# Sums of weight quarters: accumulating transfers within SBUF instead of additions on GpSimd

## The chip, the core and the metric

The kernel runs on one core of a Trainium2 chip. A core has TensorE (matrix products into PSUM), VectorE, ScalarE and GpSimd (elementwise work on the on-chip memory SBUF), and SyncE, whose queue here issues transfers. In the profile they are PE (its weight loads PEld), DVE, ACT, POOL and SP; transfers run on 16 engines that all queues share. The metric is the device time of one execution in microseconds. Three runs of the kernel before took 1261.45, 1261.13 and 1259.82 us: median 1261.13.

## The reference

One inference step of a two-layer decoder on 512 prompt tokens and 8 x 8 sample tokens, model width 1024, all in float32. Layer 0 mixes by a gated linear recurrence, layer 1 by attention with a sliding window; each layer ends in a feed-forward part, and the scales and shifts of the normalizations come from a condition vector through further matrices:

```python
def swiglu(h, w_in, w_out):
    gate, up = jnp.split(h @ w_in, 2, axis=-1)
    return (jax.nn.silu(gate) * up) @ w_out
...
        x = x + g1[:, None, :] * out
        h = modulate(rms_norm(x, norm_g[l, 1]), sh2, sc2)
        x = x + g2[:, None, :] * swiglu(h, ffn_w_in[l], ffn_w_out[l])
```

`ffn_w_in` is 1024 x 5632 (gate and up, 2816 columns each), `ffn_w_out` 2816 x 1024. The change lies in the product `h @ w_in` alone.

## The kernel before

The tokens are split into two halves h = 0, 1 of 288 columns each (256 of the prompt, 32 of the samples); activations lie with their features on the partitions. Float32 matrices are multiplied in three passes of a faster format: each operand is split into a rounded part and a remainder, and rounded times rounded, rounded times remainder and remainder times rounded are accumulated in PSUM. For a weight this split is a cast on ScalarE from a tile `raw` (the loaded weights, 4 buffers, line 539) into a tile `wh`, and a subtraction on VectorE for the remainder.

Of the 22 column tiles of `w_in` per layer the first 3 (`PLAIN`, line 1225) are multiplied plainly. The other 19 are taken as *pairs*: tile i of gate and tile i of up, each split by its upper and lower 512 rows, are the four quarters of a 2 x 2 block matrix, and the two token halves, split the same way, are the four quarters of the other. One level of a fast scheme of the Strassen-Winograd kind forms 7 products of quarters in place of 8, at the price of sums of weight quarters and of activation quarters beforehand and of products afterwards. The names of the seven weight operands are 11, 22, S1, S2, 12, S3, S4. In a pair's two `raw` tiles, r11 and r12 are the two halves of the gate's tile, r21 and r22 those of the up tile, and the sums are made in place, one after the other (lines 1284 to 1302): S1 is r21 + r22 in r22, then S3 is r11 - r21 in r21, S2 is S1 - r11 in r11, and S4 is r12 - S2 in r12. These four additions or subtractions per pair, each of 128 partitions x 512 columns, run on GpSimd (`operand`, line 1262); there are 2 x 19 x 4 = 152. After each, `operand` splits the result into one of the ten `wh` buffers (line 540), rounded part and remainder side by side. The `raw` tile of up is free again once S3 is split, that of gate once S4 is split; only then can the load of a later tile go into it.

The pairs are taken in four blocks of 2, 5, 6 and 6 (`GROUPS`, less the 3 plain tiles); after each block come 16 products with `w_out` (8 column tiles, two halves). `queue` (line 1308) lists the operands in the order 11, 22, S1, S2, 12, S3, S4; `pump` (line 1323) makes the next one as soon as one of the ten `wh` is free by the program's count. `emit` (line 1416) uses them in the order S1, S2, 12, 11 of the next pair, S3, S4, 22. `seven` (line 1339) issues a product, 4 blocks of 128 rows in 3 passes, so 12 matmuls, and then the additions that turn products into results: 11 and 12 share a PSUM bank, S2, S3 and 22 another, S1 and S4 a third. Product 11 is copied out as `p1`, S1 as `p5`; S2's bank takes `p1` and is copied to `u2`; Silu makes the gate, VectorE or GpSimd multiplies by up, and `whole` splits the result for the product with `w_out`. `quarters` (line 946) makes the sums of the activations' quarters once per layer, on VectorE, from the quarters b11, b21, b12, b22, and `two` splits them.

Beside this, in layer 0, `ada_pace` spreads the products of the condition vector over the work; their weights (512 KB at a time) are loaded on SP between the weights of the pairs.

The order of instructions on every engine comes from a planner inside the kernel. Each operation is recorded with a cost, an engine and what it reads and writes (`record`, line 430); `schedule` (line 227) then places the operations one after the other by priority, by when their inputs are ready and by when a buffer is free, and the result is emitted as the fixed order of each engine's queue. For a transfer the recorded cost is 1020 ns on GpSimd's queue, and its end is reckoned from its bytes and fixed additions; for an addition on GpSimd it is 150 ns and 2.4 ns per column. Each queue works strictly in order, and waits on semaphores for what an instruction needs.

Of the kernel before, what the change touches and what calls it, by code (L numbers as in the profile page):

```python
# [16 lines left out]
ALU = mybir.AluOpType  # L17
# [10 lines left out]
HC = 288  # L28
# [487 lines left out]
def trunk_kernel(ctx, tc, a):  # L516
    nc = tc.nc
    rec = Recorder(a["shadow"])
    V, S, G, T, Q = (Engine(rec, n, o) for n, o in (("DVE", nc.vector), ("ACT", nc.scalar), ("POOL", nc.gpsimd), ("PE", nc.tensor), ("SP", nc.sync)))
# [10 lines left out]
    def ps(pool=pmm, tag="mm"):  # L530
        cnt[0] += 1
        return rec.tile(pool, tag, NMM if tag == "mm" else (8 - NMM), RMM if tag == "mm" else 1, [P, 512], F32, f"{tag}{cnt[0]}")
# [48 lines left out]
    def split(hi, lo, v):  # L581
        S.copy(hi, v)
        V.tensor_tensor(lo, v, hi.bitcast(F32), ALU.subtract)
# [362 lines left out]
    def quarters(c):  # L946

        if c == 0:
            kinds = [tb] * 8 + [ta] * 3 + [sl] * 13
            X2["kinds"] = kinds  # L950
            for j in (2, 3, 4):
                X2[j] = [None] * 4
        b11, b21, b12, b22 = [V2[h][k] for h, k in ((0, c), (0, c + 4), (1, c), (1, c + 4))]

        def two(j, y):
            X2[j][c] = [X2["kinds"].pop(0)(F32R) for _ in range(2)]
            split(X2[j][c][0].r[:, 0:HC], X2[j][c][1].r[:, 0:HC], y.f[:, 0:HC])
            y.done()

        def minus(o, p, q):  # L960
            V.tensor_tensor(*[y.f[:, 0:HC] for y in (o, p, q)], ALU.subtract)

        minus(b11, b12, b11)
        minus(b12, b22, b12)
        two(3, b12)
        minus(b22, b22, b11)
        minus(b21, b21, b22)
        two(2, b22)
        two(4, b21)

# [26 lines left out]
    def load_more(upto=NRAW):  # L997
        while nload[0] < len(units) and nload[0] - nconv[0] < upto:
            u = units[nload[0]]
            u.raw = raws()  # L1000
            t = u.raw.f[:, 0 : u.kc * P].rearrange("p (k n) -> p k n", n=P)
            for rows, ks, cols, src in u.srcs:
                Q.dma_start(t[rows, ks, cols], src)
            nload[0] += 1
# [53 lines left out]
    def residual(h, o, c, g, last):  # L1058
        xp, xs = x[h][:, c, 0:HP], v48(x[h][:, c, HP:HC])
        V.scalar_tensor_tensor(xp, o[:, 0:HP], mp(g, c), xp, ALU.mult, ALU.add)  # L1060
        t = ta()
        V.tensor_tensor(v48(t.f[:, 0:32]), v48(o[:, HP:HC]), msam(g, c, h), ALU.mult)
        (V if g == L1 + G2 and c == KC - 1 else G).tensor_tensor(xs, xs, v48(t.f[:, 0:32]), ALU.add)
        t.done()
        if last and (g != L1 + G2 or c < KC - 1):
            square(h, c)
# [147 lines left out]
    for m in range(KC):  # L1214
# [3 lines left out]
            lambda h, o, m=m: residual(h, o, m, G1, True),  # L1218
# [8 lines left out]
    def ffn(l, g, after):  # L1227
# [18 lines left out]
        for f in range(PLAIN):  # L1246
            for w, ev in ((0, evac_gate), (1, evac_up(f))):
                c = 2 * f + w
                linear(unit_cols(wi, w * DFF + f * P), hops, ev, lambda h, c=c: quarters(c) if h == 1 and c < 4 else None)

                jobs[-1].late = f == PLAIN - 1
# [9 lines left out]

        def operand(i, name, src, sums=()):
            w = W[i, name] = whs()
            for o, p, q, op in sums:
                G.tensor_tensor(o, p, q, op)
            S.copy(w.r[:, 0:H2], src)
            V.tensor_tensor(w.r[:, H2 : 2 * H2], src, w.f[:, 0:H2], ALU.subtract)

        def steps(i):

            ug_, uu = pairs_[i]

            def views():
                if uu.raw is None:
                    load_more()
                return [u.raw.f[:, o : o + H2] for u in (ug_, uu) for o in (0, H2)]

            def a11():
                operand(i, "11", views()[0])

            def a22():
                operand(i, "22", views()[3])

            def s1():
                r11, r12, r21, r22 = views()
                operand(i, "S1", r22, [(r22, r21, r22, ALU.add)])

            def s2():
                r11, r12, r21, r22 = views()
                operand(i, "S2", r11, [(r21, r11, r21, ALU.subtract), (r11, r22, r11, ALU.subtract)])  # L1290

            def a12():
                operand(i, "12", views()[1])

            def s3():
                operand(i, "S3", views()[2])
                uu.raw.done()
                nconv[0] += 1

            def s4():  # L1300
                r11, r12, r21, r22 = views()
                operand(i, "S4", r12, [(r12, r12, r11, ALU.subtract)])
                ug_.raw.done()
                nconv[0] += 1

            return {"11": a11, "22": a22, "S1": s1, "S2": s2, "12": a12, "S3": s3, "S4": s4}

        def queue():
# [14 lines left out]
        def pump(want=lambda: True):  # L1323
            while todo and (whs.live + todo[0][0] <= 2 * NHI):
                todo.popleft()[1]()
            assert want()
            load_more()

        def right(name):

            if name in ("T2", "T3", "T4"):
                return [(p.r[:, 0:HC], q.r[:, 0:HC]) for p, q in X2[int(name[1])]]
            h, c0 = {"B11": (0, 0), "B21": (0, 4), "T1": (1, 0), "B22": (1, 4)}[name]
            v = h4r(h)
            return [(v[:, k, 0, :], v[:, k, 1, :]) for k in range(c0, c0 + 4)]
# [3 lines left out]
        def seven(i, name):  # L1339

            pump(lambda: (i, name) in W)
            w = W.pop((i, name))
            bank, ops = {"11": ("a", "B11"), "12": ("a", "B21"), "S1": ("e", "T1"), "S2": ("b", "T2"), "S3": ("b", "T3"),
                         "22": ("b", "T4"), "S4": ("e", "B22")}[name]
            b = B.setdefault(i, {})
            if bank not in b:
                b[bank] = ps()
            o = b[bank][:, 0:HC]
            first = name in ("11", "S1", "S2")
            for k, (xh, xl) in enumerate(right(ops)):  # L1350
                hi, lo = [w.r[:, q + k * P : q + (k + 1) * P] for q in (0, H2)]
                T.matmul(o, hi, xh, start=first and k == 0, stop=False, skip_group_check=True)
                T.matmul(o, hi, xl, start=False, stop=False, skip_group_check=True)
                T.matmul(o, lo, xh, start=False, stop=k == 3, skip_group_check=True)
            w.done()
            pump()
            if name == "11":
                b["p1"] = ta()
                S.copy(b["p1"].f[:, 0:HC], o)
            elif name == "S1":  # L1360
                b["p5"] = td()
                S.copy(b["p5"].f[:, 0:HC], o)
            elif name == "S2":

                V.tensor_tensor(o, o, b["p1"].f[:, 0:HC], ALU.add)
                b["p1"].done()
                b["u2"] = td()
                V.tensor_copy(b["u2"].f[:, 0:HC], o)
            elif name == "12":

                b["g"] = ta()
                S.activation(b["g"].f[:, 0:HC], o, AF.Silu)
            elif name == "S3":

                y = b["p5"].f[:, 0:HC]
                V.tensor_tensor(y, o, y, ALU.add)
            elif name == "22":

                y = b["g"].f[:, 0:HC]
                V.tensor_tensor(y, y, o, ALU.mult)  # L1380
                whole(0, i, b["g"])
                del B[i]
            else:

                y, z = b["u2"].f[:, 0:HC], b["p5"].f[:, 0:HC]
                V.tensor_tensor(y, o, y, ALU.add)
                S.activation(y, y, AF.Silu)
                G.tensor_tensor(z, y, z, ALU.mult)
                b["u2"].done()
                whole(1, i, b["p5"])  # L1390

        def whole(h, f, t):
            m = mid[h][f] = (sl(F32R), sl(F32R))
            split(m[0].r[:, 0:HC], m[1].r[:, 0:HC], t.f[:, 0:HC])
            t.done()
# [664 lines left out]
```

## Time and profile before

The profiled execution took 1260.03 us, of which the span, from the first instruction to the last, is 1258.2 us.

| | before |
|---|---|
| median of 3 runs | 1261.13 us |
| profiled execution | 1260.03 us |
| its span | 1258.2 us |
| PE busy | 1244.8 us (99%) |
| DVE busy | 883.5 us (70%) |
| ACT busy | 650.3 us (52%) |
| POOL busy | 493.1 us (39%) |
| granted clock of TensorE | 0.998 |
| transfer queue of SP | 163.45 MB, 43.1% of 16 engines |
| transfer queue of GpSimd | 0.32 MB, 0.1% of 16 engines |

Nearly every instruction is issued by the recorder, so the profile gives them one line, L489; groups are told apart by the names of the tiles they write and read (`wh<-raw` is the cast of a weight, `wh<-raw,wh` its remainder, `raw<-raw` and `raw<-raw,raw` the sums of quarters within one tile and over two). A row of groups has the count, busy us, the mean ns of one, and the idle time of the engine just before, with what ended most of it. A row of windows has, for each engine, its busy us and its number of instructions in that stretch, then the granted clock, the mean busy share of the 16 transfer engines and GB/s. A row of the timeline has start, length, engine, operation, and in brackets idle time before it.

### The profile page before, as it was taken

The page shows a single profiled execution, that of the slowest core. Times are in us where ns is not written, and L with a number is a line of the kernel's source. Part 1 is how long each engine was busy: PE and PEld are TensorE (multiplying, and loading weights), DVE is VectorE, ACT ScalarE, POOL GpSimd, SP SyncE. Part 2 cuts the span into 40 slices and gives each one's busy share as a digit, 9 for nine tenths or more (in the row PEclk, how much of TensorE's full clock was granted, in tenths as well). Part 3 has the DMA queues.
Part 4 walks back from the last instruction along what each step waited for, and adds up shares of the span by engine and source line. Part 5 has one row for each costly group of instructions (what it writes and reads, how often), then busy time and mean ns, then how long its engine had stood idle before and what let it go on. Part 6 is the DMA issues. An engine that isn't in the chain of part 4 may idle for free.

```text
span 1258.2 us, 25730 instructions
## 1 busy us (share of the span) xinstructions
PE 1244.8 (99%) x9704; PEld 1181.2 (94%) x9704; DVE 883.5 (70%) x2157; ACT 650.3 (52%) x1464; POOL 493.1 (39%) x708
## 2 busy tenths in 40 slices
PE   9999999999999999999999999999999999999997
PEld 8889899899998998999999987999999999999997
DVE  7887985875574675466669878558767658757856
ACT  4787873752352354145358678538425425524522
POOL 3475751131551552345135436110435346335511
PEclk9999999999999999999999999999999999999999
DMA  9955555516646546445424321322332323323222
GB/s 301 323 188 195 177 176 151 171 45 210 201 135 181 179 161 195 158 146 148 126 68 84 74 60 57 95 84 97 91 95 84 101 85 99 97 77 98 80 90 76
DMA packets 223982, 165.42 MB, mean 131 GB/s; under 512 B 23757, under 2 KB 209065, under 8 KB 223826
## 3 DMA queue, kind: packets, MB, share of 16 engines
q1 hardware_dynamic: 223410, 163.45, 43.1%
q8 instruction: 76, 1.25, 0.4%
q14 instruction: 48, 0.39, 0.1%
q0 software_dynamic: 448, 0.32, 0.1%
HBM read 160.85 MB, written 4.87 MB: 132 GB/s over the span
## 4 chain that ended last, share of the span: by engine, by line
PE 90%; ACT 4%; DVE 4%; POOL 1%; issue 1%; DMA 1%; ACTq 0%; SPq 0%; POOLq 0%
PE mm L489 86%; PE ada L489 4%; DVE sl L489 1%; ACT h L489 1%; ACT ta L489 1%; ACT sl L489 1%; DVE ta L489 1%; ACT tb L489 1%; DMA reg<-in_ada_w_dram 1%; DVE wh L489 1%; ACT wh L489 1%; POOL few L489 0%; ACT L489 0%; DVE x L489 0%; DVE h L489 0%
## 5 line engine op out<-in xcount | busy, mean ns | idle before, releaser
L489 PE MATMUL mm<-h,wh 128*128 128x288 f32 x4128 | 591.2, 297 | 1.1 <-ACT wh L489 0.8
L489 PEld LDWEIGHTS mm<-h,wh 128*128 128x128 f32 x4128 | 559.2, 188 | 16.0 <-issue 6.8
L489 PE MATMUL mm<-sl,wh 128*128 128x288 f32 x3218 | 463.0, 296 | 0.3 <-ACT sl L489 0.3
L489 PEld LDWEIGHTS mm<-sl,wh 128*128 128x128 f32 x3218 | 437.2, 188 | 10.0 <-issue 5.9
L489 ACT CAST wh<-raw 128x512 fp32r<-128x512 f32 (+3 forms) x388 | 267.8, 711 | 304.2 <-PE mm L489 212.3
L489 DVE TENSOR_TENSOR wh<-raw,wh 128x512 fp32r<-128x512 f32 (+3 forms) x388 | 341.5, 903 | 62.1 <-ACT wh L489 57.9
L489 POOL TENSOR_TENSOR raw<-raw 128x512 f32<-128x512 f32 x76 | 109.2, 1437 | 178.2 <-DVE wh L489 147.3
L489 POOL TENSOR_TENSOR x<-x,ta 128x32 f32<-128x32 f32 x152 | 56.3, 370 | 298.9 <-DVE ta L489 298.8
L489 DVE SCALAR_TENSOR_TENSOR x<-mm,mods,x 128x256 f32<-128x256 f32 x160 | 77.2, 483 | 132.4 <-PE mm L489 131.3
L489 POOL TENSOR_TENSOR raw<-raw,raw 128x512 f32<-128x512 f32 x76 | 112.4, 1479 | 3.5
L489 PE MATMUL mm<-tb,wh 128*128 128x288 f32 (+1 forms) x488 | 88.2, 296 | 0.7 <-DVE td L489 0.6
L489 POOL TENSOR_TENSOR td<-td,td 128x288 f32<-128x288 f32 x38 | 31.7, 834 | 113.9 <-ACT td L489 113.9
L489 PEld LDWEIGHTS mm<-tb,wh 128*128 128x128 f32 x488 | 72.6, 188 | 1.3 <-DVE td L489 0.9
L489 ACT ACTIVATE ta<-x 128x288 f32<-128x288 f32 x56 | 24.5, 443 | 67.9 <-POOL x L489 62.9
L489 PE MATMUL mm<-ta,wh 128*128 128x288 f32 (+1 forms) x254 | 55.6, 297 | 0.0
L489 DVE TENSOR_TENSOR td<-mm,td 128x288 f32<-128x288 f32 x76 | 33.6, 454 | 28.8 <-PE mm L489 28.6
L489 PE MATMUL ada<-reg,cz 128*32 128x512 f32 (+1 forms) x448 | 48.3, 552 | 0.0
L489 DVE TENSOR_TENSOR sl<-td,sl 128x288 fp32r<-128x288 f32 x50 | 38.9, 777 | 7.9 <-ACT sl L489 7.5
L489 PEld LDWEIGHTS mm<-ta,wh 128*128 128x128 f32 x254 | 41.5, 188 | 1.7 <-ACT ta L489 1.7
L489 ACT COPY td<-mm 128x256 f32<-128x256 f32 (+1 forms) x102 | 33.6, 357 | 14.0 <-PE mm L489 13.9
L489 ACT CAST sl<-ta 128x288 fp32r<-128x288 f32 x54 | 23.4, 434 | 31.7 <-DVE ta L489 29.4
L489 ACT ACTIVATE ta<-ta,stat 128x256 f32<-128x256 f32 (+2 forms) x72 | 32.5, 474 | 9.1 <-DVE stat L489 8.8
(206 smaller groups left out, 1270.0 us busy)
## 6 DMA issues: line engine op xcount, KB each, us to landing
raw<-in_ffn_w_in_dram SPq DMA_DIRECT2D x88, 512.0 KB
reg<-in_ada_w_dram SPq DMA_DIRECT2D x80, 512.0 KB
raw<-in_ffn_w_out_dram SPq DMA_DIRECT2D x32, 384.0 KB
raw<-in_ffn_w_out_dram SPq DMA_DIRECT2D x32, 320.0 KB
raw<-in_rnn_w_in_dram SPq DMA_DIRECT2D x16, 512.0 KB
reg<-in_kv_ada_w_dram SPq DMA_DIRECT2D x16, 512.0 KB
wh<-in_ada_w_dram SPq DMA_DIRECT2D x24, 256.0 KB
raw<-in_rnn_w_out_dram SPq DMA_DIRECT2D x8, 512.0 KB
```

Of the source, the lines that this page charges most:

```text
L489: self.rec.add(eng, lambda: getattr(obj, name)(*map(real, args), **{k: real(v) for k, v in kw.items()}), cost, outs, ins, func, lat, port, ...
```

## The change

In `operand` the additions on GpSimd become transfers issued from GpSimd's queue, from SBUF to SBUF, that add their source to their destination. [...] The minus signs move to the other factors: in `quarters`, VectorE's four sums of the activations' quarters get other operands and one becomes an addition, and in `seven` three additions of products become subtractions. The weight operands then are r22 + r21, r21 + r11, r11 + (r22 + r21) and r12 + r11, formed in the same place and in the same sequence as before. Nothing else in the text changes; the planner's recorded cost of the four operations per pair becomes that of a transfer, and with it the order that it writes.

```diff
-        def minus(o, p, q):
-            V.tensor_tensor(*[y.f[:, 0:HC] for y in (o, p, q)], ALU.subtract)
-
-        minus(b11, b12, b11)
-        minus(b12, b22, b12)
+        def both(o, p, q, op=ALU.subtract):
+            V.tensor_tensor(*[y.f[:, 0:HC] for y in (o, p, q)], op)
+
+        both(b11, b11, b12)
+        both(b12, b12, b22)
         two(3, b12)
-        minus(b22, b22, b11)
-        minus(b21, b21, b22)
+        both(b22, b22, b11, ALU.add)
+        both(b21, b21, b22)
...
         def operand(i, name, src, sums=()):
             w = W[i, name] = whs()
-            for o, p, q, op in sums:
-                G.tensor_tensor(o, p, q, op)
+            for o, p in sums:
+                G.dma_start(o, p, accum_op=ALU.add)
             S.copy(w.r[:, 0:H2], src)
...
-                operand(i, "S1", r22, [(r22, r21, r22, ALU.add)])
+                operand(i, "S1", r22, [(r22, r21)])
...
-                operand(i, "S2", r11, [(r21, r11, r21, ALU.subtract), (r11, r22, r11, ALU.subtract)])
+                operand(i, "S2", r11, [(r21, r11), (r11, r22)])
...
-                operand(i, "S4", r12, [(r12, r12, r11, ALU.subtract)])
+                operand(i, "S4", r12, [(r12, r11)])
...
             elif name == "S2":
-                V.tensor_tensor(o, o, b["p1"].f[:, 0:HC], ALU.add)
+                V.tensor_tensor(o, o, b["p1"].f[:, 0:HC], ALU.subtract)
...
             elif name == "S3":
                 y = b["p5"].f[:, 0:HC]
-                V.tensor_tensor(y, o, y, ALU.add)
+                V.tensor_tensor(y, o, y, ALU.subtract)
...
                 y, z = b["u2"].f[:, 0:HC], b["p5"].f[:, 0:HC]
-                V.tensor_tensor(y, o, y, ALU.add)
+                V.tensor_tensor(y, o, y, ALU.subtract)
```

## The prediction

> **What bounds the kernel now.** I read the page first (busy shares, the chain that ended last), then busy time by windows, then GpSimd's own timeline.
>
> ```profile
> span 1258.2 us, 25730 instructions
> ...
> PE 1244.8 (99%) x9704; PEld 1181.2 (94%) x9704; DVE 883.5 (70%) x2157; ACT 650.3 (52%) x1464; POOL 493.1 (39%) x708
> ...
> PE 90%; ACT 4%; DVE 4%; POOL 1%; issue 1%; DMA 1%; ACTq 0%; SPq 0%; POOLq 0%
> ...
> L489 POOL TENSOR_TENSOR raw<-raw 128x512 f32<-128x512 f32 x76 | 109.2, 1437 | 178.2 <-DVE wh L489 147.3
> ...
> L489 POOL TENSOR_TENSOR raw<-raw,raw 128x512 f32<-128x512 f32 x76 | 112.4, 1479 | 3.5
> ```
>
> TensorE is busy 99% of the span and makes 90% of the chain. The two POOL groups are the additions that the change removes, 76 + 76. GpSimd stood idle 178 us before them: it has time to spare. Windows in the stretches where pairs are multiplied (337 to 588 lies in layer 0, from 815 on in layer 1; the first two rows are for later):
>
> ```profile
> core 0: us, PE busy (x) PEld busy (x) DVE busy (x) ACT busy (x) POOL busy (x), PEclk, DMA share, GB/s
> 2.00:12.00 10.00, 10.00 (x82) 9.37 (x81) 4.75 (x21) 5.97 (x10) 4.91 (x13) 1.00 0.96 293
> 236.00:241.00 5.00, 5.00 (x39) 4.76 (x39) 2.47 (x8) 1.24 (x4) 3.65 (x6) 1.00 0.47 134
> 337.00:374.00 37.00, 37.00 (x281) 35.39 (x280) 27.81 (x48) 19.32 (x41) 21.44 (x16) 1.00 0.55 168
> 438.00:484.00 46.00, 46.00 (x350) 42.79 (x349) 33.94 (x54) 23.48 (x49) 25.91 (x20) 1.00 0.56 178
> 542.00:588.00 46.00, 46.00 (x349) 42.79 (x349) 33.09 (x51) 23.64 (x48) 25.85 (x20) 1.00 0.49 148
> 943.00:988.00 45.00, 45.00 (x342) 45.00 (x341) 34.81 (x57) 23.52 (x50) 26.79 (x20) 1.00 0.26 75
> 1031.00:1086.00 55.00, 55.00 (x417) 55.00 (x416) 42.65 (x70) 29.38 (x61) 32.90 (x24) 1.00 0.30 82
> 1139.00:1192.00 53.00, 53.00 (x402) 53.00 (x402) 41.81 (x65) 29.74 (x62) 33.21 (x24) 1.00 0.27 75
> 815.00:943.00 128.00, 126.49 (x948) 125.14 (x947) 87.57 (x196) 63.44 (x140) 30.13 (x41) 1.00 0.31 94
> 1245.00:1258.20 13.20, 6.26 (x50) 5.69 (x48) 5.94 (x22) 3.28 (x6) 2.11 (x5) 0.84 0.26 89
> ```
>
> TensorE never pauses in them; one matmul passes every 55.00/417 = 0.132 us, so a product of a pair (4 blocks, 3 matmuls each) takes 12 x 0.132 = 1.58 us and a pair's seven 11.1 us. The change can gain nothing here. It can only cost, by delivering an operand late. The last-but-one row holds the start of layer 1's pairs, where TensorE is idle 1.51 us; the last is the tail, idle 6.94 us.
>
> **The change, part by part.** GpSimd's timeline over two pairs shows the chain that is replaced:
>
> ```profile
> 1044.31 1.30 POOL L489 TENSOR_TENSOR raw<-raw 128x512 f32<-128x512 f32 x1 [2.81 <-DVE wh L489]
> 1045.56 0.83 POOL L489 TENSOR_TENSOR td<-td,td 128x288 f32<-128x288 f32 x1
> 1046.33 3.28 POOL L489 TENSOR_TENSOR raw<-raw,raw 128x512 f32<-128x512 f32 x2
> 1050.81 1.61 POOL L489 TENSOR_TENSOR raw<-raw 128x512 f32<-128x512 f32 x1 [1.20 <-DVE wh L489]
> 1055.72 1.30 POOL L489 TENSOR_TENSOR raw<-raw 128x512 f32<-128x512 f32 x1 [3.30 <-DVE wh L489]
> ...
> 1066.71 1.30 POOL L489 TENSOR_TENSOR raw<-raw 128x512 f32<-128x512 f32 x1 [2.67 <-DVE wh L489]
> ```
>
> One sum for S1, two for S2, one for S4; pairs follow 11.0 us apart. Removed: 221.6 us of GpSimd's busy time. Added: 152 transfers, issued at some 0.55 us each (rows below), 84 us. GpSimd is relieved and VectorE meets it less often at their common port, both worth nothing while TensorE has no gap; if TensorE's 1.51 us went altogether, that would be the gain. The edits to signs (VectorE and the second addition of the activations' quarters) keep number, engine and size: zero.
>
> What counts is the time L from issuing one accumulating transfer to its sum being usable. The four are a strict chain, since each reads what the one before wrote or must not overwrite what it still reads, and GpSimd waits for a landing before it issues the next. Nothing in this trace accumulates by transfer. The nearest rows are GpSimd's own plain transfers, from the listing of issues (last number: median us to landing) and of their durations (ns):
>
> ```profile
> sl<-in_state_conv_dram POOLq DMA_DIRECT2D x2, 48.0 KB, 6.9
> out_sample_conv_dram<-raw POOLq DMA_DIRECT2D x2, 48.0 KB, 1.8
> ...
> L489 POOL DMA_DIRECT2D out_sample_conv_dram<-raw x2: 517/566/614, 236.3 to 236.9; - x2
> ```
>
> So 1.8 us with the transfer engines about half busy (236 to 241), 6.9 us in the opening stretch at share 0.96. The opening row gives 293/0.96 = 305 GB/s when all 16 engines work: 256 KB take 0.86 us as a plain copy, 48 KB 0.16. Low bound: 1.8 - 0.16 + 0.86 = 2.5 us (an addition as cheap as a copy). I take two copies, because a sum reads two operands for each write: 1.8 - 0.16 + 1.72 = 3.4 us. High bound: 6.9 + 1.6 = 8.5 us. Sharing with the weights' loads, if engines then give each half: layer 1, share 0.28, the 1.72 grows by 1/(0.72 + 0.14) to 2.0, L = 3.6; if the sums get only what is left over, 1.72/0.72 = 2.4, L = 4.0; taken 3.9. Layer 0, share 0.53: 1.72/0.735 = 2.3 to 1.72/0.47 = 3.7, L = 4.0 to 5.3; taken 4.55.
>
> The Trainium skill ("Collectives: The Full Stack", the section on the bandwidth ceiling) says that reducing halves throughput because it reads two sources per write, not because adding costs time; no run here shows it yet. Its page "DMA: Bandwidth & Descriptors", section "Anatomy of one DMA", fits a GpSimd transfer as 2.0 us plus bytes over 436 GB/s, an estimated 2.6 us for 256 KB; the trace's 1.8 us for 48 KB lies a little under that, and by it no sum would be late (the 1264 us below).
>
> How much L is hidden: `wh` has ten buffers, one per operand. Operands are made in the order 11, 22, S1, S2, 12, S3, S4 and used as S1, S2, 12, next pair's 11, S3, S4, 22. Operand 22 of pair i+1, after which its chain starts, gets a buffer when S3 of pair i-1 is through; nine products then stand ahead of S1(i+1), ten ahead of S2, fourteen ahead of S4: 14.3, 15.8 and 22.2 us. These steps use these rows:
>
> ```profile
> L489 DVE TENSOR_TENSOR wh<-raw,wh 128x512 fp32r<-128x512 f32 x266 | 211.2, 826 | 49.1 <-ACT wh L489 46.2
> L489 ACT CAST wh<-raw 128x512 fp32r<-128x512 f32 x266 | 157.7, 620 | 164.1 <-PE mm L489 100.6 <-POOL raw L489 53.9 <-DMA raw<-in_ffn_w_in_dram 4.1
> ...
> L489 ACT COPY td<-mm 128x288 f32<-128x288 f32 x38 | 15.1, 398 | 9.0 <-PE mm L489 9.0
> L489 ACT COPY ta<-mm 128x288 f32<-128x288 f32 x42 | 16.7, 399 | 33.4 <-PE mm L489 33.4
> ```
>
> S2 needs 22's cast and remainder (0.62 + 0.69, the remainder without GpSimd beside it), 3 L, its own two (1.31) and six handovers of some 0.1 us (an estimate): 3.2 + 3 L <= 15.8, L <= 4.2. S4 needs 3.3 + 4 L <= 22.2, L <= 4.7. So S2 is late first, at 4.2 us. (Before, the same chain used 3 x 1.45 and left 8 us.) Behind a late S2 cast ScalarE's queue holds the reads of PSUM and Silu, behind a late landing GpSimd's queue holds the gating product `td` and the residual sums `x`, and a late S4 holds a `raw` pair and so the next load on SP. All lengthen the same wait.
>
> Layer 1: 3.9 < 4.2, nothing late. Layer 0: 4.55 - 4.2 = 0.35 us, three times per pair, for the pairs that the output products between blocks don't cover. Blocks have 2, 5, 6 and 6 pairs, two of each later one are prepared ahead, 3 + 4 + 4 = 11 remain: 0.35 x 3 x 11 = 12 us. Cross-check by load: four sums of 1.72 us in 11.1 us add 0.62 to the shares 0.55, 0.56, 0.49, which oversubscribes the engines by 0.17, 0.18, 0.11: at most 37 x 0.17 + 46 x 0.18 + 46 x 0.11 = 20 us if no load can slip into the output products. 12 lies inside.
>
> Then the order. The planner allows an accumulating transfer about three times what it allowed an addition, and writes another order: sums of two pairs alternate on GpSimd, casts of sums come later. That has a price at any L. In layer 1's first pair S2's cast now stands on ScalarE right behind the read of S1's PSUM, whose product S2 follows directly on TensorE: a wait of 0.40 + 0.62 + three handovers + what of the remainder's 0.69 two matmuls don't cover (0.43), 1.7 us. In two later blocks product 12 comes directly after 11 in the same bank, with ScalarE's copy (0.40) and two handovers between: 2 x 0.6. Together 2.9 us, which the order before does not have.
>
> Sum: profiled execution 1260.0 (span 1258.2 and 1.8 around it) + 12 + 2.9 = 1275; the median of the runs lies 1.1 above that execution: 1276 us.
>
> **The rivals.**
> Hidden anyway: if a sum costs little more than a copy, L is 2.5 to 3.3 everywhere, only the order's 2.9 stays: 1264. For it: the 1.8 us row. Against: the second read.
> Chain-bound in both layers: at L = 6 (nearer the 6.9 row) S2 is late by 3 x 1.8 = 5.4 us in 11 pairs of each layer: 5.4 x 22 = 119, with the order 1383; L = 5 gives 53, 1317. Against: the 6.9 us had a full queue of loads ahead.
> GpSimd held up while it writes transfers: if VectorE's instructions (busy 42.65 of 55.00) block it, an issue waits on average 0.78 x 0.35 = 0.27 us, L in layer 0 4.8, 20 us late instead of 12, layer 1 at the edge: 1284. Against: issuing took 0.52 to 0.61 us with VectorE half busy. The skill's "SBUF — State Buffer", section "Who interferes with whom", has VectorE's two-port modes lock GpSimd out, but not tensor_tensor, which is what VectorE does here; by that rule this rival falls.
> Faster: the relieved GpSimd and the new order close TensorE's gaps at the start of layer 1's pairs (1.51 us) and take a few tenths from the tail's 6.94: with no order's waits, 1261.1 - 1.5 - 1.5 = 1258. It decides if no sum is late and more than 2.5 us of the idle 13.4 goes.
>
> **How the numbers follow.** My forecast (late in layer 0 alone, 1266 to 1295) 0.40, hidden 0.24, chain-bound 0.22, GpSimd held up 0.05, faster 0.09. About 0.2% (2.5 us) is what a measurement here can tell. Faster 0.09; of hidden, whose 2.9 us lies at that edge, half is within 0.2%: 0.12; slower 0.79. The range leaves out the faster case and the half of chain-bound beyond L = 5.4: 1259 to 1340.
>
> **What the profile after would show.** Right: POOL's raw groups gone, 152 issues of about 0.55 us; landings of 3.4 to 5 us; ScalarE's cast waiting for a transfer (DMA raw) instead of POOL raw; TensorE below 100% in 337 to 588, near 100% in layer 1 but for the three order waits. Landings under 4 us and no idle in layer 0: hidden anyway. Landings above 5 us, windows of layer 1 below 95%: chain-bound. Issues well over 0.6 us: GpSimd held up. What would make me wrong most is the price of the addition in the transfer engines, of which no row here tells.

## The result, and the profile after

The changed kernel takes 1332.72 us (median of 3 runs, 1328.62 to 1337.56) against 1261.13: a ratio of 1.057, 95% interval 1.051 to 1.063. The loss is 71.6 us, where the prediction had 15. The profiled execution took 1328.62 us, its span is 1326.8, which is 68.6 us more than before.

The page of the changed kernel: span, busy time, the queue of GpSimd's transfers (packets, MB, share of 16 engines), the chain that ended last by engine, the groups of ScalarE's casts and of the new transfers, and the landing of these:

```profile
span 1326.8 us, 25870 instructions
...
PE 1270.2 (96%) x9704; PEld 1191.5 (90%) x9704; DVE 834.0 (63%) x2157; ACT 646.0 (49%) x1464; POOL 409.6 (31%) x708
...
q0 software_dynamic: 22336, 40.18, 17.6%
...
DMA 10%; PE 8%; issue 4%; POOL 1%; ACT 1%; DVE 1%; ACTq 0%; POOLq 0%
...
L489 ACT CAST wh<-raw 128x512 fp32r<-128x512 f32 (+3 forms) x388 | 267.4, 710 | 355.5 <-DMA raw<-raw 193.0
...
L489 POOL DMA_DIRECT2D raw<-raw x152 | 132.1, 891 | 364.3 <-DMA raw<-raw 218.2
...
raw<-raw POOLq DMA_DIRECT2D x152, 256.0 KB, 4.6
```

The chain of the page accounts for only about a quarter of the span (its shares sum to 25%), so nothing is read from it here. GpSimd's additions are gone, and the group that replaces them, 152 issues, costs GpSimd 0.89 us each where 0.55 was forecast. Both GpSimd (218 us) and ScalarE's casts (193 us) now stand idle for a landing. TensorE's share is down to 96%. The same six windows as in the prediction, same columns (the same times; the work in them is what the kernel before did up to some 60 us earlier):

```profile
337.00:374.00 37.00, 33.98 (x238) 31.23 (x237) 19.05 (x41) 14.95 (x32) 9.99 (x12) 0.95 0.77 183
438.00:484.00 46.00, 38.58 (x270) 35.80 (x270) 20.29 (x39) 17.21 (x37) 12.30 (x15) 0.93 0.86 205
542.00:588.00 46.00, 41.95 (x312) 38.52 (x311) 18.07 (x42) 11.06 (x21) 12.08 (x21) 0.98 0.60 161
943.00:988.00 45.00, 44.81 (x337) 44.57 (x338) 27.95 (x64) 13.97 (x25) 11.67 (x21) 1.00 0.53 137
1031.00:1086.00 55.00, 52.08 (x380) 50.45 (x379) 30.34 (x70) 17.54 (x33) 15.34 (x25) 1.00 0.61 142
1139.00:1192.00 53.00, 49.76 (x367) 48.59 (x368) 27.42 (x59) 16.05 (x29) 13.21 (x23) 1.00 0.57 139
```

TensorE has gaps in both layers. In layer 0 the granted clock drops as well, to as little as 0.93, where before it was 1.00 in all six. The time from the start of the issue to the landing, over the transfers of a stretch without pairs' products (900 to 940), of layer 0 (300 to 670) and of layer 1 (940 to 1300):

```profile
DMA to landing us min/median/max: 3.3/3.3/3.8
...
DMA to landing us min/median/max: 3.2/5.3/8.9
...
DMA to landing us min/median/max: 3.3/4.5/7.1
```

The quiet 3.3 us is what the prediction had built from a copy and a second read (3.4). In the layers it had taken 4.55 and 3.9.

To split the loss, take the moment at which SP issues layer 1's first load of the feed-forward matrix, from SP's timeline, first the kernel before, then the changed one:

```profile
808.74 50.25 SPq L489 DMA_DIRECT2D raw<-in_ffn_w_in_dram  x9
```

```profile
849.67 9.45 SPq L489 DMA_DIRECT2D raw<-in_ffn_w_in_dram  x3
```

So 40.9 us are lost up to there, which is taken as layer 0, and 68.6 - 40.9 = 27.7 us after it, in layer 1. This split is made for every run below (landings in us):

| run | median us | lost in layer 0 | in layer 1 | landing, layer 0 | layer 1 |
|---|---|---|---|---|---|
| changed kernel | 1332.7 | 40.9 | 27.7 | 5.3 | 4.5 |
| no_sums | 1265.4 | 2.1 | 3.6 | - | - |
| plain_copy | 1274.9 | 6.1 | 4.0 | 3.8 | 2.4 |
| half_bytes | 1281.5 | 18.6 | 3.6 | 4.1 | 2.8 |
| threeq_bytes | 1303.3 | 28.2 | 13.7 | 4.8 | 3.5 |
| light_ada | 1298.6 | 10.0 | 24.7 | 4.3 | 4.4 |
| s2_gpsimd | 1289.2 | 19.6 | 1.3 | 4.8 | 3.7 |
| s2_light | 1266.9 | 8.1 | 1.2 | 3.7 | 3.7 |
| s4_only | 1268.5 | 5.2 | 3.1 | 4.2 | 4.2 |
| told_late | 1339.5 | 46.8 | 35.5 | 4.7 | 4.2 |
| order_only | 1310.9 | 25.4 | 28.3 | - | - |
| old_order | 1580.2 | 180.5 | 140.2 | 3.6 | 3.3 |

(The splits are of the profiled execution, against that of the kernel before. In most runs it lies within 3 us of the median; in the changed kernel, `light_ada`, `plain_copy` and `s2_gpsimd` it was 4, 4, 5 and 8 us faster than the median, so their losses are a little larger in a typical execution. Landings are medians over the transfers between 300 and 670 and between 940 and 1300 us; in `old_order`, which is 320 us longer, these stretches hold only parts of the two layers.)

One place of layer 0 shows the mechanism. Rows of three engines' timelines of the changed kernel (start, length, and in brackets the idle time before and what ended it), then, in a fence of their own, three windows, the first of them within the wait:

```profile
465.86 0.86 POOL L489 DMA_DIRECT2D raw<-raw  x1 [4.09 <-DVE wh L489]
467.60 0.85 POOL L489 DMA_DIRECT2D raw<-raw  x1 [0.88 <-DMA raw<-raw]
...
474.82 0.87 POOL L489 DMA_DIRECT2D raw<-raw  x1 [5.48 <-DMA raw<-raw]
...
474.61 0.62 ACT L489 CAST wh<-raw 128x512 fp32r<-128x512 f32 x1 [5.10 <-DMA raw<-raw]
...
476.43 0.85 PE L489 MATMUL mm<-tb,wh 128*128 128x288 f32 x2 [5.65 <-ACT wh L489]
```

```profile
470.00:475.00 5.00, 0.78 (x6) 0.55 (x5) 0.00 (x1) 0.39 (x1) 0.18 (x1) 0.83 1.01 265
476.40:480.00 3.60, 3.57 (x15) 3.58 (x16) 0.69 (x1) 0.68 (x2) 1.27 (x2) 0.50 1.02 213
480.00:484.00 4.00, 4.00 (x31) 4.00 (x31) 1.99 (x5) 2.02 (x5) 0.72 (x1) 0.98 0.72 133
```

Two sums are issued at 465.86 and 467.60, and GpSimd and ScalarE go on only at 474.8 and 474.6, seven to nine us later, while the transfer engines are full (share 1.01 in the first window; shares near 1 come out a little over it here). SP had begun to issue four loads of 512 KB for the condition vectors at 460.47. TensorE waits 5.65 us for the cast. Then it has a second loss: 15 matmuls in 3.60 us at a granted clock of 0.50, against 31 in the next 4.00 us.

### The profile page after: what moved, and what is told of

Same layout as the page of the kernel before. It is cut to its first block, busy times and chain, and to the rows that moved or that the text cites. A ratio compares the mean times of both kernels' runs of the same rounds, so it can differ in the third digit from the quotient of the medians.

```text
span 1326.8 us, 25870 instructions
## 1 busy us (share of the span) xinstructions
PE 1270.2 (96%) x9704; PEld 1191.5 (90%) x9704; DVE 834.0 (63%) x2157; ACT 646.0 (49%) x1464; POOL 409.6 (31%) x708
## 3 DMA queue, kind: packets, MB, share of 16 engines
q1 hardware_dynamic: 223410, 163.45, 40.9%
q8 instruction: 76, 1.25, 0.4%
## 5 line engine op out<-in xcount | busy, mean ns | idle before, releaser
L489 PE MATMUL mm<-h,wh 128*128 128x288 f32 x4128 | 602.0, 299 | 16.9 <-ACT wh L489 12.4
L489 DVE TENSOR_TENSOR wh<-raw,wh 128x512 fp32r<-128x512 f32 (+3 forms) x388 | 310.5, 812 | 195.2 <-ACT wh L489 192.3
L489 POOL DMA_DIRECT2D raw<-raw x152 | 132.1, 891 | 364.3 <-DMA raw<-raw 218.2
L489 POOL TENSOR_TENSOR x<-x,ta 128x32 f32<-128x32 f32 x152 | 64.0, 421 | 257.9 <-DVE ta L489 257.8
L489 PE MATMUL mm<-tb,wh 128*128 128x288 f32 (+1 forms) x488 | 96.6, 307 | 26.1 <-ACT wh L489 16.1
L489 ACT ACTIVATE td<-td 128x288 f32<-128x288 f32 x38 | 16.9, 444 | 46.5 <-DVE td L489 46.4
L489 DVE TENSOR_TENSOR mm<-mm,ta 128x288 f32<-128x288 f32 x38 | 17.6, 464 | 33.6 <-PE mm L489 33.5
```

The source lines that it names most:

```text
L489: self.rec.add(eng, lambda: getattr(obj, name)(*map(real, args), **{k: real(v) for k, v in kw.items()}), cost, outs, ins, func, lat, port, ...
```

## Experiments

Theory 1: the loss is that of sums that are usable too late, because a transfer that adds takes longer than the products ahead of its operand give. Rivals: the new order itself; the crowding of the weights' loads; a planner that was told the wrong time. All edits are against the changed kernel. Where one has `G.record(..., emit=...)` or `Q.record(..., emit=...)`, the planner reckons with the recorded operation and the `emit` function is issued in its place; the lines that give `record` this argument are left out of the cuts shown.

### The order alone

**GpSimd's additions in the new order** (`order_only`): the planner reckons with a transfer, an addition is emitted.

```diff
-                G.dma_start(o, p, accum_op=ALU.add)
+                G.record("dma_start", (o, p), {"accum_op": ALU.add},
+                         emit=lambda o=o, p=p: nc.gpsimd.tensor_tensor(real(o), real(o), real(p), ALU.add))
```

> GpSimd adds as it did before (each sum o = o + p on GpSimd itself), but the planner is still told of a transfer, so every engine's order is the changed kernel's, instruction by instruction. The theory of late sums: the sums are there after 1.5 us instead of 5, so only the waits built into the order remain, which I put at 2.9 us: 1262 to 1267 us. The rival that the new order is the main cost: 1300 us and more, with TensorE idle in both layers as in the changed kernel.

Measured: 1310.9 us (ratio 1.037 to 1.041), a miss for theory 1. But it isn't the order alone that differs. VectorE's remainder in this run, and what TensorE waited for between 250 and 1290 us (us in total, times, longest):

```profile
L489 DVE TENSOR_TENSOR wh<-raw,wh 128x512 fp32r<-128x512 f32 x266 | 234.3, 900 | 59.2 <-ACT wh L489 58.9
```

```profile
PE mm L489 <- DVE wh L489: 25.2, 21, 3.5
```

The remainder takes 0.90 us (0.83 before), and what TensorE waits for last is VectorE. The casts, which come between a sum and its remainder, stand idle for GpSimd's additions for only 12.1 us in this run (53.9 before), so it isn't directly that the sums are late: the additions stand elsewhere in this order and run beside VectorE's work. So the order had to be tried with nothing in the place of the sums.

**The order with no sums** (`no_sums`):

```diff
-                G.dma_start(o, p, accum_op=ALU.add)
+                G.record("dma_start", (o, p), {"accum_op": ALU.add}, emit=lambda: None)
```

> After's order, planned with the transfers, but nothing is issued for the sums: S1, S2 and S4 are taken from plain quarters, so the products of those three are wrong, and GpSimd and the transfer engines have nothing to do for them. Theory 1 (the order costs the 2.9 us of its three waits, everything else of the +72 us comes from landings that are late): 1261 to 1267 us, TensorE above 98%. Rival (the order itself, made for slow sums, costs tens of us whatever a sum takes, as the 1310.9 us of the same order with GpSimd's additions suggests): 1285 to 1320 us.

Measured: 1265.4 us (ratio 1.002 to 1.004). TensorE's timeline, the rows with idle time in layer 1's pairs, and VectorE's remainder:

```profile
904.06 0.53 PE L489 MATMUL mm<-tb,wh 128*128 128x288 f32 x2 [1.06 <-ACT wh L489]
904.79 0.40 PE L489 MATMUL mm<-tb,wh 128*128 128x288 f32 x1 [0.19 <-DVE wh L489]
989.64 0.80 PE L489 MATMUL mm<-h,wh 128*128 128x288 f32 x4 [0.49 <-ACT ta L489]
...
1077.99 0.80 PE L489 MATMUL mm<-h,wh 128*128 128x288 f32 x4 [0.49 <-ACT ta L489]
```

```profile
L489 DVE TENSOR_TENSOR wh<-raw,wh 128x512 fp32r<-128x512 f32 x266 | 179.6, 692 | 84.7 <-ACT wh L489 83.6
```

These are the three waits that the prediction had named: 1.25 us in the first pair (forecast 1.7) and twice 0.49 (0.6). The order costs about 4 us, and the other 68 of the 71.6 come with the transfers. The row of VectorE shows one more thing: relieved of GpSimd, its remainder falls from 0.83 to 0.69 us, and the kernel gains nothing by it. (The Trainium skill, "SBUF — State Buffer", section "Who interferes with whom", has a VectorE instruction with two inputs in SBUF contend with a GpSimd instruction that reads SBUF; the 0.69, 0.83 and 0.90 us agree.) What made `order_only` 45 us slower than `no_sums` lies in the additions themselves at those places; VectorE's lengthened remainders are the wait that the profile names, but no run separates them from GpSimd's queue. So the order is cheap with no sums in it, but it was not with additions on GpSimd.

**The transfers in the old order** (`old_order`): the planner reckons with an addition, the transfer is emitted.

```diff
-                G.dma_start(o, p, accum_op=ALU.add)
+                G.record("tensor_tensor", (o, o, p, ALU.add), {},
+                         emit=lambda o=o, p=p: nc.gpsimd.dma_start(real(o), real(p), accum_op=ALU.add))
```

> The sums are accumulating transfers, but the planner is told of additions on GpSimd, so the order is that of the kernel before. The theory of late sums: the transfers land as late as in the changed kernel (median 4.5 to 5.3 us) in an order that leaves them only 1.4 us, so ScalarE's and GpSimd's queues are held up by them as well: as slow as the changed kernel or slower, 1335 to 1400 us. The rival that the order is the main cost: 1260 to 1285 us.

Measured: 1580.2 us (ratio 1.251 to 1.254), beyond the range given. The longest waits:

```profile
ACT wh L489 <- DMA raw<-raw: 488.6, 113, 11.5
DVE wh L489 <- ACT wh L489: 455.4, 136, 11.3
```

The landings are short here (3.6 and 3.3 us), yet the loss is the largest of all: each cast stands in ScalarE's queue where an addition's sum would have been there, ScalarE waits at it for the landing, and everything behind it waits too. The new order saves 247 us of what this one costs.

**A planner told the truth** (`told_late`):

```diff
-                op.end = b + op.lat + 1700
+                op.end = b + op.lat + (1700 if op.eng == "SP" or op.lat < 700 else 2900)
```

> The change with one number of the planner altered: it is told that a 256 KB transfer lands 1.2 us later than before, some 5.3 us after its issue begins, which is what the trace shows for layer 0. Everything is computed. Theory 1 (three landings one after the other need more time than the products between them give, so no order hides them): 1310 to 1345 us, as before the edit. Rival (the loss is that of an order made for landings that are too early): 1265 to 1295 us.

Measured: 1339.5 us (ratio 1.060 to 1.064), as theory 1 has it. Knowing the 5.3 us doesn't help the planner. Its landings are even shorter than the changed kernel's (4.7 and 4.2 us) and its loss is larger, so the median landing alone doesn't set the loss: where each order puts the sums counts too.

### What the landing is made of

**The same transfers without adding** (`plain_copy`; the sums are then wrong, copies of one quarter):

```diff
-                G.dma_start(o, p, accum_op=ALU.add)
+                G.record("dma_start", (o, p), {"accum_op": ALU.add},
+                         emit=lambda o=o, p=p: nc.gpsimd.dma_start(real(o), real(p)))
```

> The same transfers in the same order, but they copy and don't add, so the weight operands are wrong: only the price of the addition in the transfer engines goes. The theory of late sums, with the price in the second read: landings 0.7 us earlier on quiet engines (2.5 instead of 3.2 us) and half the load on the engines, so medians under 4.2 us in layer 1 and near it in layer 0: 1275 to 1300 us. If the fixed part of a transfer and the waiting behind the loads make the landing late, and the addition does not: 1315 us and more.

Measured: 1274.9 us (ratio 1.008 to 1.013), the lower end of the first range. The group of issues, and layer 1's queue of GpSimd with its landing (940 to 1300):

```profile
L1266 POOL DMA_DIRECT2D raw<-raw x152 | 84.4, 556 | 281.2 <-DMA raw<-raw 139.0
```

```profile
q0 software_dynamic: 5440, 17.83, 13.1%
...
raw<-raw POOLq DMA_DIRECT2D x68, 256.0 KB, 2.4
```

The same two rows of the changed kernel, same stretch:

```profile
q0 software_dynamic: 10250, 18.64, 30.2%
...
raw<-raw POOLq DMA_DIRECT2D x70, 256.0 KB, 4.5
```

A copy takes 0.131 x 360/68 = 0.69 us of all 16 engines, a sum 0.302 x 360/71 = 1.53 (18.64 MB are the bytes of 71 sums; one was issued before the stretch), 2.2 times as much. So the rule of the Trainium skill ("Collectives: The Full Stack", the section on the bandwidth ceiling) that reducing halves throughput agrees with the trace here. The issue grows too: 0.56 us for a copy, 0.89 for a sum, in the same order beside the same VectorE. That goes with the form of the transfer; the rival in which VectorE holds GpSimd up would have lengthened both. In the quiet stretch (900 to 940) an adding issue takes 0.85 us and more as well. The skill's "DMA: Bandwidth & Descriptors" (section "Anatomy of one DMA") with its estimated 2.6 us describes the copy (2.4 in layer 1), not the sum.

**Fewer bytes** (`half_bytes`, 256 of 512 columns, and `threeq_bytes`, 384):

```diff
-                G.dma_start(o, p, accum_op=ALU.add)
+                G.record("dma_start", (o, p), {"accum_op": ALU.add},
+                         emit=lambda o=o, p=p: nc.gpsimd.dma_start(real(o)[:, 0:256], real(p)[:, 0:256], accum_op=ALU.add))
```

> After's order, each transfer sums only 256 of the 512 columns (the other half of each sum is wrong), so the data time of one falls from 1.53 to some 0.77 us and the load on the transfer engines by sums is halved; number, issue (0.87 us) and the wait before the first packet when the engines are quiet (1.65 us with the issue) stay. Theory 1 (bytes: data time and the crowding that the sums themselves make): landings from issue of 3.3 to 4.0 us, under the 4.2 us at which S2 is late, 1262 to 1285 us. Rival (the fixed part and the queue behind the weights' loads dominate): landings in layer 0 stay at 4.5 us or more, 1290 to 1320 us.

> After's order, each transfer sums 384 of the 512 columns (the last quarter of each sum is wrong). With 256 columns the landings were 2.8 us in layer 1 and 4.1 us in layer 0 and the time 1281.5; with 512 they were 4.5 and 5.3 and 1332.7. Here, half way, some 3.7 and 4.7 us. Theory 1 (nothing is late in layer 1 until a landing takes 4.2 us): layer 1 stays whole, TensorE at 98% or more between 1000 and 1200 us, layer 0 takes all of the loss, 1288 to 1303 us. Rival (the loss grows evenly with the bytes, without a threshold): half way in both layers, TensorE at about 97% there, 1304 to 1312 us.

Measured: 1281.5 us (ratio 1.014 to 1.017), inside theory 1's range though layer 0's landing of 4.1 us is a little over its 4.0, and 1303.3 us (1.031 to 1.036). TensorE between 1000 and 1200 us, in layer 1, of `half_bytes`, of `threeq_bytes` and of the changed kernel:

```profile
1000.00:1200.00 200.00, 198.96 (x1496) 197.98 (x1495) 116.85 (x244) 82.33 (x167) 62.31 (x89) 1.00 0.52 119
```

```profile
1000.00:1200.00 200.00, 196.05 (x1459) 193.40 (x1458) 114.68 (x240) 79.82 (x162) 58.52 (x84) 1.00 0.58 130
```

```profile
1000.00:1200.00 200.00, 189.21 (x1383) 183.66 (x1382) 108.85 (x226) 75.04 (x150) 56.76 (x81) 1.00 0.62 140
```

With half the bytes layer 1 loses no more than with no sums at all (3.6 us both). With three quarters it already loses 10 us more than that, at a median landing of 3.5 us, so the threshold that theory 1 puts at 4.2 is not there: TensorE's 98.0% lies at the edge of what theory 1 gave, the time at the edge of both ranges. The loss in layer 1 is 0, 10 and 24 us more than that of `no_sums` at median landings of 2.8, 3.5 and 4.5: it begins somewhere between 2.8 and 3.5 us and grows by about 14 us per us of landing from there. (The busy share understates the loss: the changed kernel's window has 1383 matmuls, 8% fewer than the 1502 of `no_sums` in the same window, while its share is 5% lower.)

**Lighter loads beside them** (`light_ada`): the condition vectors' weights, 512 KB at a time, cut to 64 KB from the third group on; TensorE's work keeps its size, because its matmuls read the 128 loaded columns four times (that part of the edit is not shown); the scales are wrong.

```diff
-        Q.dma_start(b.f, w[k * P : (k + 1) * P, o + i * D : o + (i + 1) * D])
+        src = w[k * P : (k + 1) * P, o + i * D : o + (i + 1) * D]
+        small = src if u < 16 else w[k * P : (k + 1) * P, o + i * D : o + i * D + P]
+        dst = b.f if u < 16 else b.f[:, 0:P]
+        Q.record("dma_start", (b.f, src), {}, emit=lambda: nc.sync.dma_start(real(dst), small))
...
```

> Order and sums as in the changed kernel, but from the third group on the loads for the condition vector's matrices bring 64 KB in place of 512 KB (TensorE then uses these columns four times over, so scales and shifts are wrong). If what delays the sums in layer 0 is the traffic beside them, layer 0's landings fall from 5.3 to about 4.5 us, layer 1's value, and its loss of 41 us to about 20: 1305 to 1315 us, layer 1 unchanged. If the landing time doesn't depend on that traffic: 1330 us.

Measured: 1298.6 us (ratio 1.027 to 1.031), more gained than expected. These loads run in layer 0 alone, and the table shows it: there the landing falls from 5.3 to 4.3 us and the loss from 40.9 to 10.0, while layer 1 keeps 24.7 of 27.7. So three quarters of layer 0's loss goes with these loads. It goes by way of the sums and not of the pairs' own weights: between 300 and 670 us ScalarE's casts stand idle 52.8 us for a sum's landing where the changed kernel has 110.3, and 8.1 us for a load of `ffn_w_in` where it has 11.5. And at the same landing layer 0 (4.3 us) loses less than layer 1 (4.4). A reason would be the condition vectors' products, which are further cover there; no run tests it. Their row in the kernel before, 300 to 660 us:

```profile
L489 PE MATMUL ada<-reg,cz 128*32 128x512 f32 x208 | 25.0, 598 | 0.0
```

### The chain of three

**S2's two sums on GpSimd again** (`s2_gpsimd`, shown), **that with the lighter loads** (`s2_light`), and **S4's sum alone as a transfer** (`s4_only`, with the condition turned round to `"S4"`). In these three the planner reckons with what is issued, so it also writes another order than the changed kernel's:

```diff
-                G.dma_start(o, p, accum_op=ALU.add)
+                if name == "S2":
+                    G.tensor_tensor(o, o, p, ALU.add)
+                else:
+                    G.dma_start(o, p, accum_op=ALU.add)
```

> The two sums of S2 are GpSimd additions again, those of S1 and S4 (76 of 152) stay transfers; everything is computed. Theory 1 (a chain of three landings ahead of S2): now one landing and two additions, 3.2 + 5.3 + 2.9 = 11.4 us against 15.8, S4 at 3.3 + 2 x 5.3 + 2.9 = 16.8 against 22.2: nothing late, 1260 to 1270 us. Rival (the load that the sums put on the transfer engines, which also delays the weights): half of the transfers, about half of the loss, 1285 to 1305 us.

> The two sums of S2 on GpSimd and the condition vectors' loads cut to 64 KB as well (the scales are wrong). With S2 on GpSimd alone layer 1 was whole and layer 0 still lost some 12 us in a few waits. Theory 1 (those are single landings that stand behind a burst of loads on the transfer engines, the longest 9.4 us from issue): 1261 to 1270 us. Rival (the additions left on GpSimd meet VectorE at the common port, or the order costs it): 1276 to 1292 us, as without the cut.

> Only S4's sum is a transfer (38 of 152), S1's and S2's stay GpSimd additions; everything is computed. S4 is the sum with the most products ahead of it. Theory 1: 3.3 + 3 x 1.45 + L <= 22.2 us holds up to L = 14 us, no landing seen so far is longer than 9.4 us, nothing is late: 1259 to 1266 us. Rival (GpSimd waits in its queue for the landing, and the next pair's additions behind it come late, in layer 0 above all): 1270 to 1290 us. If it comes out below the kernel before, it is the form in which the change could be kept.

Measured: 1289.2 us (ratio 1.020 to 1.024), 1266.9 (1.004 to 1.007) and 1268.5 (1.004 to 1.008). Windows of `s2_gpsimd`, layer 0 and layer 1:

```profile
300.00:660.00 360.00, 347.45 (x2586) 324.36 (x2585) 207.69 (x413) 132.03 (x266) 114.45 (x143) 0.99 0.65 180
...
1000.00:1200.00 200.00, 199.81 (x1511) 199.58 (x1510) 130.57 (x248) 84.38 (x169) 74.75 (x87) 1.00 0.52 123
```

Layer 1 is whole with half of the transfers, although each still takes 3.7 us, more than the 3.5 with which `threeq_bytes` lost 13.7 us there: the length of one landing doesn't decide it. That the number of landings in a row does is the reading that fits, but the order differs too, and no run separates the two. In layer 0 the run missed theory 1's 1260 to 1270 and came out inside the rival's 1285 to 1305; `s2_light`, which met its 1261 to 1270, says that the loads beside the sums are why. With them a single landing takes up to 9.4 us, with the lighter loads at most 6.1, and most of the loss goes. `s4_only` is slower than the kernel before by about 7 us, 5.2 of the 8.3 us of its profiled execution in layer 0: between the 1266 at which theory 1's range ends and the 1270 at which the rival's begins, so it decides for neither. No version with transfers came out at or below the kernel before, in which TensorE, 99% busy, has nearly nothing to gain.

## Why the prediction was right and wrong

The direction was right: TensorE at 99% could only lose, and it lost by operands that come late. The place was half right: layer 0 was to lose alone, but 27.7 of the 68.6 us are lost in layer 1. Step by step:

- **What can be gained: nothing.** Right. `no_sums` takes all of the sums' work off GpSimd and a sixth off VectorE's remainders, and is not faster than before.
- **The order, 2.9 us.** Right: 2.2 us in the three places named, about 4 us in all.
- **A sum costs two copies, 3.4 us when quiet.** Right: 3.3 us, and 1.53 us of the engines' time against the 1.72 taken. That the total fits so well is partly luck: the shortest landings with 256, 384 and 512 columns, 2.6, 2.9 and 3.2 us, put what grows with the bytes at some 1.2 us (an estimate from these three) and the fixed part at 2.0, where the prediction had 1.72 and 1.64.
- **Issue of 0.55 us.** Wrong for an adding transfer: 0.89. The quiet 3.3 us contains it. Issues well over 0.6 us were to be the sign of GpSimd held up; the sign came, but from the transfer itself, as `plain_copy` shows.
- **L beside the loads, 4.55 in layer 0 and 3.9 in layer 1, "nothing late" there.** This is the step that failed first. Measured are 5.3, the upper bound, and 4.5, above the bound of 4.0. The growth had been worked out from mean shares over tens of us, but a sum meets what is queued when it is issued, a burst of loads or another sum. `light_ada` shows the first in layer 0 (5.3 to 4.3 us without the bursts), `half_bytes` that in layer 1 it is mainly the sums' own bytes (4.5 to 2.8). How the engines divide their time between two queues no run shows.
- **Late by three times L - 4.2, in 11 pairs per layer.** With the measured medians this gives 3 x 11 x 1.1 = 36 us and 3 x 11 x 0.3 = 10, in all 1260 + 46 + 2.9 = 1309 for the profiled execution of 1328.6. So the size of L accounts for 34 of the 54 us missing there, and the formula itself for the other 20. It took one L for all landings, where they spread from 3.2 to 8.9 us, and a late one need not be paid back by an early one. Its threshold was too high in layer 1 (3.5 us already costs 10) and probably too low in layer 0 (it left out the 25.0 us of condition vectors' products, 1.5 us for each of 17 pairs). That the 36 us of layer 0 come near its measured loss is therefore partly chance; the measured loss also holds the next term, which the formula doesn't have.
- **The clock** had no term. In layer 0 TensorE's longest waits are each followed by a stretch at half clock (last section). The mean granted clock fell from 0.998 to 0.991, which is 0.009 x 1326.8 - 0.002 x 1258.2 = 9 us of TensorE's time, part of it inside the waits.

Of the rivals, the chain-bound one with its L = 5 (1317 us) was nearest. Of its signs, layer 1 below 95% came (94.6% between 1000 and 1200); landings above 5 us came in layer 0 alone (5.3, in layer 1 4.5). Hidden anyway falls by the 2.2 copies, GpSimd held up by the comparison of issues, faster by `no_sums`.

What stays open, beside the 45 us of `order_only`, is the threshold in layer 1. The waits of GpSimd there, 940 to 1300 us in the changed kernel, suggest a reason:

```profile
POOL raw L489 <- DMA raw<-raw: 94.9, 42, 5.3
...
POOL raw L489 <- DVE wh L489: 21.0, 10, 6.6
```

GpSimd's queue holds the sums of two pairs in turn and waits for a landing 42 times in 17 pairs, two or three times per pair, and ten times for the remainder that frees the next pair's first sum. Then not only the cover in buffers counts, but also how often per pair of 11.1 us the queue can come round: three landings of 3.5 us and a remainder with its handovers are about that. No run tells this apart from the spread of the landings.

## What to carry over

To move an addition from an idle engine into the transfer queues, count the landings in a row beside the bytes: here each was an issue of 0.89 us, a queue and 2.2 times a copy's time on the engines, and everything behind its consumer in an in-order queue waits with it. Take the landing's spread beside the real loads as the price, since the mean over a layer hides the bursts, and look at what GpSimd, one queue, must wait for per round. Where the bound engine is at 99%, relieving the others buys nothing, and each gap that is opened may cost more than its own length.

## What the runs showed of the hardware that was not expected

- An adding transfer is dearer to issue than a plain one of the same shape: 0.89 against 0.56 us of GpSimd's time.
- It moves in smaller packets: between 940 and 1300 us the queue has 10250/71 = 144 packets per sum, 5440/68 = 80 per copy of the same 256 KB.
- Half clock comes after short waits. In the changed kernel's layers TensorE waits five times for 2.3 us or more (2.34, 2.32, 5.65, 2.99 and 4.04 us, all in layer 0), and the 3.3 to 3.6 us after each run at a granted clock of 0.50 to 0.57; after its waits of 1.1 to 1.8 us the clock stays at 1.00, and layer 1 has no longer ones. The length alone doesn't decide: in `s2_gpsimd` half clock follows a wait of 1.96 us (0.52) and doesn't follow one of 2.20 (1.00). The row that follows a wait of 2.34 us, and the window behind it:

```profile
349.98 0.53 PE L489 MATMUL mm<-tb,wh 128*128 128x288 f32 x2 [2.34 <-ACT wh L489]
```

```profile
350.00:354.00 4.00, 4.00 (x18) 4.00 (x19) 1.87 (x5) 0.77 (x2) 1.28 (x2) 0.57 0.82 193
```

18 matmuls in 4.00 us, where 30 pass at full clock (0.132 us each). The Trainium skill ("TensorE: Matmul & The Clock Gate", Part 1) has the clock halve after at least one idle window of about 3.4 us, in windows that run freely; here 2.34 us of idle time by the profile were enough.
